# Placing the first pass over the third last chunk between the two negations of the last big chunk, in an elementwise kernel on one core

## The chip, the cores and the metric

One core of a Trainium2 chip. The metric is the device time of one execution in microseconds; lower is better. Most executions of a kernel here agree within about 2 us.

## The reference

```python
pred = np.clip(pred, 1e-7, 1 - 1e-7)                # both inputs 8192 x 8192, float32
return -(target * np.log(pred) + (1 - target) * np.log(1 - pred))   # target is 0 or 1
```

Since the target is 0 or 1, the kernel computes |t - 1 + p|, which is p or 1 - p, takes one logarithm and negates it.

## The kernel before

The data are cut into 37 chunks of 128 partitions. Chunks 2 to 33 hold 15360 elements per partition; 0, 1, 34 and 35 hold half of that (7680); 36 holds 2048. Two big places in a ring for pred (which is overwritten by the result) and for target take turns. A front is a clip and a subtraction on VectorE, then abs and logarithm on ScalarE; a back is the negation on VectorE. Big chunks are worked in two halves. In the profiles L82 is the clip, L85 the subtraction, L88 the abs, L89 the logarithm, L93 the negation, L74 and L78 the issue of a pred load and of a store. All engines run their instructions in the order of the program.

```python
def load(k):
    queue = nc.sync if k == 0 else nc.gpsimd
    nc.gpsimd.dma_start(out=spot(ring_t, k), in_=chunk(target, k))     # casts to bf16
    queue.dma_start(out=spot(ring_p, k), in_=chunk(pred, k))

def store(k):
    queue = nc.sync if k >= n - 3 else nc.gpsimd
    queue.dma_start(out=chunk(out, k), in_=spot(ring_p, k))

def front(k, *part):
    p, t = spot(ring_p, k, *part), spot(ring_t, k, *part)
    nc.vector.tensor_scalar(out=p, in0=p, scalar1=EPS, scalar2=1 - EPS, op0=Alu.max, op1=Alu.min)
    nc.vector.scalar_tensor_tensor(out=p, in0=t, scalar=1.0, in1=p, op0=Alu.subtract, op1=Alu.add)
    nc.scalar.activation(out=p, in_=p, func=Act.Abs)
    nc.scalar.activation(out=p, in_=p, func=Act.Ln)

def back(k, *part):
    p = spot(ring_p, k, *part)
    nc.vector.tensor_scalar(out=p, in0=p, scalar1=-1.0, scalar2=None, op0=Alu.mult)

# ... the first chunks cut ...
for k in range(2, n - 3):                  # n = 37
    front(k, (0, 2)); front(k, (1, 2))     # on two lines in the kernel
    back(k, (0, 2));  back(k, (1, 2))
    # ... store(k) and the loads that follow it, for k < n - 4 ...
store(n - 4)
a, b, c = n - 3, n - 2, n - 1
front(a)
front(b, (0, 2)); front(b, (1, 2))
back(a); store(a)
front(c)
back(b); store(b)
back(c); store(c)
```

Of the kernel before, what the change touches and what calls it, by code (L numbers as in the profile page):

```python
# [1 line left out]

# [4 lines left out]

EPS = 1e-7





BIG = 15 * 1024
HALF = BIG // 2


def plan(total):

    n, last = divmod(total, BIG)  # L20
    assert n > 4 and 0 < last <= 2048
    spots = [(HALF, 0), (HALF, HALF)]
    spots += [(BIG, k % 2 * BIG) for k in range(1, n - 1)]
    end = (n - 1) % 2 * BIG
    return spots + [(HALF, end), (HALF, end + HALF), (last, 2 * BIG)]



@with_exitstack
def kernel(  # L30
    ctx: ExitStack,
    tc: tile.TileContext,
    pred: bass.AP,
    target: bass.AP,
    out: bass.AP,
):






    nc = tc.nc
    fp32 = mybir.dt.float32
    bf16 = mybir.dt.bfloat16
    Alu = mybir.AluOpType
    Act = mybir.ActivationFunctionType
    P = nc.NUM_PARTITIONS

    R, C = pred.shape  # L50
    spots = plan(R * C // P)
    n = len(spots)
    widths = [w for w, _ in spots]
    cols = [sum(widths[:k]) for k in range(n)]

    def chunk(ap, k):
        flat = ap.rearrange("r c -> (r c)")
        return flat[cols[k] * P : (cols[k] + widths[k]) * P].rearrange("(p w) -> p w", p=P)

    pool = ctx.enter_context(tc.tile_pool(name="rings", bufs=1))  # L60
    ring = [P, 2 * BIG + widths[-1]]
    ring_p = pool.tile(ring, fp32, name="ring_p", tag="ring_p")
    ring_t = pool.tile(ring, bf16, name="ring_t", tag="ring_t")
    warm = pool.tile([1, 8], fp32, name="warm", tag="warm")

    def spot(ring, k, part=(0, 1)):
        w, c = spots[k]
        i, m = part
        return ring[:, c + i * w // m : c + (i + 1) * w // m]

    def load(k):
        queue = nc.sync if k == 0 else nc.gpsimd
        nc.gpsimd.dma_start(out=spot(ring_t, k), in_=chunk(target, k))  # L73
# [8 lines that stand above are left out]
        nc.vector.tensor_scalar(  # L82
            out=p, in0=p, scalar1=EPS, scalar2=1 - EPS, op0=Alu.max, op1=Alu.min
        )
        nc.vector.scalar_tensor_tensor(  # L85
            out=p, in0=t, scalar=1.0, in1=p, op0=Alu.subtract, op1=Alu.add
# [6 lines that stand above are left out]
        nc.vector.tensor_scalar(out=p, in0=p, scalar1=-1.0, scalar2=None, op0=Alu.mult)  # L93

    with tc.manual_schedule():
        for k in range(3):
            load(k)
        nc.vector.memset(warm, 1.0)  # L98
        nc.scalar.activation(out=warm, in_=warm, func=Act.Ln)  # L99
        front(0)  # L100
        front(1)
        back(0)
        store(0)
        back(1)
        store(1)
        load(3)
        for k in range(2, n - 3):
            front(k, (0, 2))
            front(k, (1, 2))
            back(k, (0, 2))  # L110
            back(k, (1, 2))
            if k < n - 4:
                store(k)

                for j in range(k + 2, n if k == n - 5 else k + 3):
                    load(j)
        store(n - 4)
        a, b, c = n - 3, n - 2, n - 1
        front(a)
        front(b, (0, 2))  # L120
        front(b, (1, 2))
        back(a)
        store(a)
        front(c)
        back(b)
        store(b)
        back(c)
        store(c)


# [1 line left out]
_INS = ['pred', 'target']  # L132
_OUTS = [((8192, 8192), 'float32')]


# [23 lines left out]
```

## Time and profile before

| | before |
|---|---|
| time, median of 3 runs (later 6) | 1867.1 us (1867.5) |
| VectorE / ScalarE busy | 60% / 48% |
| moved to and from HBM | 805 MB, 432 GB/s |
| VectorE waiting for pred loads, whole run | 391.0 us |

How to read it: no compute engine is near full, and the DMA engines hardly rest until the last 17 us. So a wait of a compute engine costs time only if the DMA engines run dry for it. The page (the profile's summary), the busy shares by 2 us stretches and the timeline that carry this are shown in the prediction.

### The profile page before, as it was taken

The page shows a single profiled execution, that of the slowest core. Times are in us where ns is not written, and L with a number is a line of the kernel's source. Part 1 is how long each engine was busy: PE and PEld are TensorE (multiplying, and loading weights), DVE is VectorE, ACT ScalarE, POOL GpSimd, SP SyncE. Part 2 cuts the span into 40 slices and gives each one's busy share as a digit, 9 for nine tenths or more (in the row PEclk, how much of TensorE's full clock was granted, in tenths as well). Part 3 has the DMA queues.
Part 4 walks back from the last instruction along what each step waited for, and adds up shares of the span by engine and source line. Part 5 has one row for each costly group of instructions (what it writes and reads, how often), then busy time and mean ns, then how long its engine had stood idle before and what let it go on. Part 6 is the DMA issues. An engine that isn't in the chain of part 4 may idle for free.

```text
span 1865.4 us, 619 instructions
## 1 busy us (share of the span) xinstructions
DVE 1122.2 (60%) x210; ACT 899.9 (48%) x142; POOL 60.9 (3%) x111
## 2 busy tenths in 40 slices
DVE  4655767555576655557665555766555576755575
ACT  3345553335555334555543355553345555433556
POOL 0000000000000000000000000000000000000010
DMA  9999999999999999999999999999999999999998
GB/s 295 376 358 340 357 341 365 387 379 353 344 353 353 359 387 381 351 353 345 353 360 387 385 350 353 345 353 361 383 386 349 354 350 345 362 383 387 356 329 379
DMA packets 15988, 671.13 MB, mean 360 GB/s; under 512 B 1776, under 2 KB 1776, under 8 KB 1904
## 3 DMA queue, kind: packets, MB, share of 16 engines
q0 software_dynamic: 15408, 658.25, 98.4%
q1 hardware_dynamic: 576, 12.85, 1.7%
q14 instruction: 4, 0.03, 0.0%
HBM read 536.87 MB, written 268.44 MB: 432 GB/s over the span
## 4 chain that ended last, share of the span: by engine, by line
DMA 36%; ACT 24%; issue 23%; DVE 16%; POOL 1%; DVEq 0%; POOLq 0%; PEldq 0%
DMA ring_p<-in_pred_dram 33%; ACT ring_p L88 12%; ACT ring_p L89 12%; DVE ring_p L85 8%; DVE ring_p L82 4%; DVE ring_p L93 4%; DMA out_dram<-ring_p 3%; POOL ring_t L73 0%; POOL out_dram L78 0%; DVEq L154 0%; POOLq L78 0%; DVEq L85 0%; PEldq L154 0%; POOLq L74 0%; POOLq L73 0%
## 5 line engine op out<-in xcount | busy, mean ns | idle before, releaser
L88 ACT ACTIVATE ring_p<-ring_p 128x7680 f32<-128x7680 f32 (+1 forms) x70 | 450.6, 6437 | 948.2 <-DVE ring_p L85 948.2
L85 DVE SCALAR_TENSOR_TENSOR ring_p<-ring_t,ring_p 128x7680 f32<-128x7680 bf16 (+1 forms) x70 | 557.2, 7960 | 2.4
L82 DVE TENSOR_SCALAR ring_p<-ring_p 128x7680 f32<-128x7680 f32 (+1 forms) x70 | 284.0, 4057 | 391.0 <-DMA ring_p<-in_pred_dram 391.0
L93 DVE TENSOR_SCALAR ring_p<-ring_p 128x7680 f32<-128x7680 f32 (+1 forms) x69 | 284.0, 4117 | 336.2 <-ACT ring_p L89 336.2
L89 ACT ACTIVATE ring_p<-ring_p 128x7680 f32<-128x7680 f32 (+1 forms) x70 | 451.1, 6444 | 2.2
L78 POOL DMA_DIRECT2D out_dram<-ring_p x34 | 21.6, 635 | 841.0 <-DVE ring_p L93 841.0
L74 POOL DMA_DIRECT2D ring_p<-in_pred_dram x36 | 19.3, 535 | 909.5 <-DMA out_dram<-ring_p 909.5
L73 POOL DMA_DIRECT2D ring_t<-in_target_dram x37 | 20.3, 550 | 0.8 <-PEq L154 0.8
L99 ACT ACT_TABLE_LOAD x1 | 1.3, 1283 | 0.7 <-PEq L143 0.7
L98 DVE MEMSET warm<- 1x8 f32 x1 | 0.1, 65 | 0.8 <-PEq L143 0.8
L99 ACT ACTIVATE warm<-warm 1x8 f32<-1x8 f32 x1 | 0.2, 208 | 0.0
L143 POOL MEMSET const-float32-0.0<- 128x1 f32 x1 | 0.1, 98 | 0.2 <-issue 0.2
L143 POOL MEMSET const-bfloat16-1.0<- 128x1 bf16 x1 | 0.1, 101 | 0.0
L143 POOL MEMSET const-float32-1.0<- 128x1 f32 x1 | 0.1, 98 | 0.0
L143 POOL MEMSET const-uint8-127<- 128x1 uint8 x1 | 0.1, 98 | 0.0
## 6 DMA issues: line engine op xcount, KB each, us to landing
ring_p<-in_pred_dram POOLq DMA_DIRECT2D x32, 7680.0 KB, 35.9
out_dram<-ring_p POOLq DMA_DIRECT2D x32, 7680.0 KB, 29.2
ring_t<-in_target_dram POOLq DMA_DIRECT2D x32, 3840.0 KB, 46.8
ring_p<-in_pred_dram POOLq DMA_DIRECT2D x3, 3840.0 KB, 35.0
ring_t<-in_target_dram POOLq DMA_DIRECT2D x4, 1920.0 KB, 27.6
out_dram<-ring_p POOLq DMA_DIRECT2D x2, 3840.0 KB, 27.6
out_dram<-ring_p SPq DMA_DIRECT2D x2, 3840.0 KB, 12.2
ring_p<-in_pred_dram SPq DMA_DIRECT2D x1, 3840.0 KB, 18.6
```

The source lines that it names most:

```text
L73: nc.gpsimd.dma_start(out=spot(ring_t, k), in_=chunk(target, k))
L74: queue.dma_start(out=spot(ring_p, k), in_=chunk(pred, k))
L78: queue.dma_start(out=chunk(out, k), in_=spot(ring_p, k))
L82: nc.vector.tensor_scalar(out=p, in0=p, scalar1=EPS, scalar2=1 - EPS, op0=Alu.max, op1=Alu.min)
L85: nc.vector.scalar_tensor_tensor(out=p, in0=t, scalar=1.0, in1=p, op0=Alu.subtract, op1=Alu.add)
L88: nc.scalar.activation(out=p, in_=p, func=Act.Abs)
L89: nc.scalar.activation(out=p, in_=p, func=Act.Ln)
L93: nc.vector.tensor_scalar(out=p, in0=p, scalar1=-1.0, scalar2=None, op0=Alu.mult)
L98: nc.vector.memset(warm, 1.0)
L99: nc.scalar.activation(out=warm, in_=warm, func=Act.Ln)
L143: nc = _bacc.Bacc("TRN2", target_bir_lowering=False, num_devices=1)
```

## The change

Its intent: VectorE has nothing to do while ScalarE finishes the second half of chunk 33. Let it do the front of 34 in that time, so that ScalarE gets the last chunks sooner and the last stores start sooner. The memset of a warm-up tile also moves ahead of the loads.

```diff
     with tc.manual_schedule():
+        nc.vector.memset(warm, 1.0)
         for k in range(3):
             load(k)
-        nc.vector.memset(warm, 1.0)
@@
-        for k in range(2, n - 3):
+        for k in range(2, n - 4):
@@ (store(k) and its loads lose their condition)
-        store(n - 4)
-        a, b, c = n - 3, n - 2, n - 1
+        z, a, b, c = range(n - 4, n)
+        front(z, (0, 2))
+        front(z, (1, 2))
+        back(z, (0, 2))
         front(a)
+        back(z, (1, 2))
+        store(z)
         front(b, (0, 2))
```

More of the change, by code (lines that the diff above doesn't have):

```diff
@@ L111 @@
             back(k, (1, 2))
-            if k < n - 4:
-                store(k)
-                for j in range(k + 2, n if k == n - 5 else k + 3):
-                    load(j)
-        store(n - 4)
-        a, b, c = n - 3, n - 2, n - 1
+            store(k)
+            for j in range(k + 2, n if k == n - 5 else k + 3):
+                load(j)
+        z, a, b, c = range(n - 4, n)
+        front(z, (0, 2))
+        front(z, (1, 2))
+        back(z, (0, 2))
         front(a)
+        back(z, (1, 2))
+        store(z)
         front(b, (0, 2))
```

## The prediction

> **What bounds the kernel now.** I read the page first: the busy shares, the 40 slices, then the end of the timeline, then the DMA transfers and their busy share by stretch.
>
> ```profile
> DVE 1122.2 (60%) x210; ACT 899.9 (48%) x142; POOL 60.9 (3%) x111
> DMA  9999999999999999999999999999999999999998
> HBM read 536.87 MB, written 268.44 MB: 432 GB/s over the span
> ```
>
> No compute engine is more than 60% busy, while the DMA row shows a nine in every slice but the last. The data are fixed (805 MB), so the kernel is bound by its 16 DMA engines, and a reordering of VectorE can only win what the DMA engines lose by standing idle. The place to look is the end, where the last digit is an 8. The busy share by 2 us stretches shows one hole:
>
> ```profile
> 1848.00:1850.00 2.00, 2.00 (x1) 1.97 (x2) 0.00 (x0) 1.00 0.36 154
> 1850.00:1852.00 2.00, 2.00 (x2) 1.06 (x1) 0.00 (x0) 1.00 0.04 15
> 1852.00:1854.00 2.00, 0.65 (x1) 0.00 (x0) 0.00 (x0) 1.00 1.17 492
> ```
>
> The last two columns are DMA share and GB/s. After it the stores of the last two chunks run at full rate to the end. Why the hole is there shows in the timeline:
>
> ```profile
> 1797.53 6.60 ACT L89 ACTIVATE ring_p<-ring_p 128x7680 f32<-128x7680 f32 x1
> 1804.17 4.16 DVE L93 TENSOR_SCALAR ring_p<-ring_p 128x7680 f32<-128x7680 f32 x1 [8.97 <-ACT ring_p L89]
> 1808.24 4.15 DVE L82 TENSOR_SCALAR ring_p<-ring_p 128x7680 f32<-128x7680 f32 x1
> 1808.62 3.90 POOL L78 DMA_DIRECT2D out_dram<-ring_p  x1 [22.23 <-DVE ring_p L93]
> 1812.43 8.16 DVE L85 SCALAR_TENSOR_TENSOR ring_p<-ring_t,ring_p 128x7680 f32<-128x7680 bf16 x1
> 1820.62 6.61 ACT L88 ACTIVATE ring_p<-ring_p 128x7680 f32<-128x7680 f32 x1 [16.49 <-DVE ring_p L85]
> ...
> 1847.35 5.29 DVE L93 TENSOR_SCALAR ring_p<-ring_p 128x7680 f32<-128x7680 f32 x2 [5.84 <-ACT ring_p L89]
> ```
>
> Chunks count from 0 to 36: 33 is the last big one, 34 and 35 the halves (third and second last), 36 the small one. VectorE idles 8.97 us for ScalarE before the second negation of 33, and only then begins 34; ScalarE idles 16.49 us for that, and is then busy without a break to the end of 36. So the negation of 35 comes only at 1847.35 to 1851.51, its store reaches the engines at 1852.37, and DMA engines that finished earlier had nothing to do.
>
> How much of the hole counts is a question of the single DMA engine. The trace's DMA records show fixed packet times (61440 B of store 33: 2.267 us; 30720 B of stores 34 and 35: 1.138; 8192 B of store 36: 0.31), eight packets of each transfer per engine, and a steady lag between the engines: p36 (the pred load of chunk 36) completes on the first engine at 1820.25 and on the last at 1824.63. At the hole most engines run out at 1848.1, others near 1850, the last at 1851.53. The mean idle per engine is about 3.3 us (from 0.36 and 0.04 over four microseconds, 3.2), but for the last engine it is 1852.37 - 1851.53 = 0.84 us.
>
> **What the Trainium skill says.** "DMA: Bandwidth & Descriptors", Issuing engines are not separate DMA queues: DMAs of all issuers run on the same 16 engines. The trace agrees: store 34, on the SyncE queue, interleaves with store 33, on the GpSimd one, from 1838.9, and the sum stays at 16 engines. So an earlier store adds no bandwidth; it only fills idle time. "SBUF — State Buffer", Who interferes with whom: a VectorE `tensor_scalar` in its two-port mode and a GpSimd access lock each other out for a whole instruction, which delays the descriptors of GpSimd's DMAs. The trace agrees: the issue of store 33 took 3.90 us, to 1812.52, just after the clip ended at 1812.39, where an issue beside the two-input subtraction took 0.53 (1783.75). This matters, since the change moves that issue. "Perfetto Trace Analysis", What "DMA-bound" means, lists as one bound the specific DMA engines; the lag above is of that kind, and it sets how much of the hole pays.
>
> **The change part by part.** The warm-up memset moves ahead of the loads in the program, but it is on VectorE and they are on other queues; it ran at 0.80 us, long before the first data at 19.3. Worth 0. Splitting the loop at k = n - 4 adds and removes no instruction. What is left is one swap on VectorE: front(34) before the second negation of 33.
>
> I re-run the end with the measured durations. VectorE ends the first negation of 33 at 1795.2. front(34) needs p34, issued at 1783.75 and landed 17.8 us later:
>
> ```profile
> ring_p<-in_pred_dram POOLq DMA_DIRECT2D x1, 3840.0 KB, 17.8
> ```
>
> That is 1801.6, so the new first wait is on a load, 6.4 us, inside the 8.97 us that VectorE idled anyway. Clip 1801.6 to 1805.8, subtraction to 1814.0. Then the second negation of 33, whose ScalarE input was ready at 1804.13: 1813.9 to 1818.1, where before it ended at 1808.3. The store of 33 is issued at about 1818.4 instead of 1808.62, and its descriptors are written by about 1819 instead of 1812.5, since the next clip can start only when p35 lands at 1819.8 and does not lock GpSimd out.
>
> Does that late store cost? The GpSimd queue drains in order, and the loads of 34 to 36 stand ahead of it. The first engine came to store 33 at 1819.9, the last finished p36 at 1824.3. Descriptors ready at 1819 to 1821 may leave the early engines idle for up to a microsecond or so; the late ones, which set the end, don't wait. Cost on the path: 0.
>
> What the earlier front(34) gives: ScalarE starts 34 at 1814.0 instead of 1820.62 and ends it at 1827.2 instead of 1833.9. Front(35) first half waits for p35: 1819.8 to 1826.1; second half to 1832.4, only 0.7 earlier than before. Negation of 34: 1832.4 to 1836.5, store issued at 1836.6 instead of 1838.08. ScalarE has 35 at 1827.2 to 1840.6 without a gap (four passes of 3.4), so the negation of 35 runs 1840.7 to 1844.8 instead of 1847.35 to 1851.51: 6.7 us earlier. 36 follows: ScalarE to 1844.4, negation by 1846.0. Both last stores are thus in the queue before the first engine runs out at 1848.1, and the hole closes.
>
> The gain is what the last engine idled. Its work from the landing of p36 on: 8 x 2.267 (store 33) + 8 x 1.138 (34) + 8 x 1.138 (35) + 8 x 0.3135 (36) = 18.14 + 9.10 + 9.10 + 2.51 = 38.85 us, so 1824.63 + 38.85 = 1863.5. As a check the same sum for 33 and 34 alone gives 1851.87, and store 34 landed at 1851.88. Store 36 landed at 1864.56 before, so 1.1 us less by this sum; 0.84 by the idle time alone. I take 0.95: 1867.1 - 0.95 = 1866.15, rounded to 1866.2. The 6.7 us won on ScalarE are nearly all hidden behind the transfers.
>
> **The rivals.** *The whole hole pays.* If engines shared one limit, so that late ones sped up when early ones rest, the mean idle of 3.3 us would be won: 1863.8. Against it: a packet of 30720 B takes 1.138 us (median of 1.141 on the SyncE queue), full house or not, and the lag among the engines stands at 4.4 us from 515 us on and never closes. *The late store of 33 opens a hole of its own.* GpSimd's first transfer was issued at 1.23 us and its first packet ran at 5.57, so up to 4.3 us from issue to packet on an empty queue: 1818.4 + 4.3 = 1822.7, still 1.6 us before the last engine is free. But if the issue collides with the clip of 35 (to 1822.0) on top of that, packets start near 1826 and the last engine loses about 2 us; less the 0.95 won, that makes 1868.2. For it: 3.90 us for that very issue before. Against it: 1.4 us between the issue and the landing of p35. *Nothing at all:* where the lag of the last engine happens to meet the store, or run-to-run spread (1866.34 to 1867.97 before) swallows it: 1867.1.
>
> **Range and chances.** The spread of before is as large as the gain. I centre on 1866.2 and go from 1864.6 (half of the hole paying, with a fast run) to 1867.8 (gain lost to a collision or a slow draw). 2% is 37 us; the hole is 3.3 and the whole stretch that the change touches lasts 60, all but the hole filled with transfers. So within 2% is all but certain.
>
> **What would show it.** After the change: VectorE's wait before the clip of 34 is on p34, about 6.4 us, and ScalarE's wait of 16.49 shrinks to about 10; store 33 issued near 1818.4 in about half a microsecond; store of 35 issued near 1845; no stretch under 0.9 DMA share from 1848 to 1854; end of the span near 1864.4. I am wrong in mechanism if the issue of store 33 takes microseconds again with a dip of DMA share near 1821 to 1824 that reaches the last engine, or if p34 lands later than 1802. I am wrong in size if the engines' lag at the end is gone and the span falls by 3 us.

## More of the kernel before

One more view before, the sums of waits from 1780 us on, is of use for the comparison (waiting line, what it waited for, us in total, times, longest):

```profile
ACT ring_p L88 <- DVE ring_p L85: 44.5, 2, 28.0
...
POOL out_dram L78 <- DVE ring_p L93: 22.2, 1, 22.2
DVE ring_p L93 <- ACT ring_p L89: 16.6, 4, 9.0
```

VectorE's line has no wait for a load there: it waits for ScalarE's logarithms instead, 16.6 us.

## The result, and the profile after

1865.84 us, median of 6 runs (1865.15 to 1866.23), against 1867.5 (1866.34 to 1868.11) for 6 runs of before. A ratio here is the mean time of one kernel's runs over that of the other's of the same rounds, so not quite the ratio of the medians quoted; it is 0.9991 with a 95% interval from 0.9978 to 1.0004. The six times of the changed kernel all lie below the six of before, so a small gain is likely, but the interval doesn't exclude none, and what the gain comes from can't be told from the times. The traces tell it.

The stretches of the changed kernel at the place of the hole (the last two columns are DMA share and GB/s):

```profile
1848.00:1850.00 2.00, 0.00 (x0) 0.00 (x0) 0.00 (x0) 1.00 1.07 461
1850.00:1852.00 2.00, 0.00 (x0) 0.00 (x0) 0.00 (x0) 1.00 1.03 445
1852.00:1854.00 2.00, 0.00 (x0) 0.00 (x0) 0.00 (x0) 1.00 0.89 384
```

DMA share of 0.36 and 0.04 has become 1.07 and 1.03: the hole is closed. (A share can pass 1, or fall to 0.89 with no engine idle, since the profile counts the whole of a packet in the stretch in which it starts.) Its timeline:

```profile
1801.49 4.16 DVE L82 TENSOR_SCALAR ring_p<-ring_p 128x7680 f32<-128x7680 f32 x1 [6.53 <-DMA ring_p<-in_pred_dram]
1805.69 8.16 DVE L85 SCALAR_TENSOR_TENSOR ring_p<-ring_t,ring_p 128x7680 f32<-128x7680 bf16 x1
1813.76 4.15 DVE L93 TENSOR_SCALAR ring_p<-ring_p 128x7680 f32<-128x7680 f32 x1
1813.88 6.61 ACT L88 ACTIVATE ring_p<-ring_p 128x7680 f32<-128x7680 f32 x1 [9.98 <-DVE ring_p L85]
1818.21 0.54 POOL L78 DMA_DIRECT2D out_dram<-ring_p  x1 [31.94 <-DVE ring_p L93]
1819.62 2.16 DVE L82 TENSOR_SCALAR ring_p<-ring_p 128x3840 f32<-128x3840 f32 x1 [1.70 <-DMA ring_p<-in_pred_dram]
...
1840.62 5.29 DVE L93 TENSOR_SCALAR ring_p<-ring_p 128x7680 f32<-128x7680 f32 x2 [0.85 <-ACT ring_p L89]
```

The first line is the clip of 34, now waiting for its load and not behind a negation; the third is the delayed second negation of 33, and the fifth the store of 33, issued 9.6 us later than before but in 0.54 us instead of 3.90. The last line, the negations of 35 and 36, starts at 1840.62 instead of 1847.35. The sums of waits from 1780 us on:

```profile
ACT ring_p L88 <- DVE ring_p L85: 38.0, 2, 28.0
POOL out_dram L78 <- DVE ring_p L93: 31.9, 1, 31.9
...
DVE ring_p L82 <- DMA ring_p<-in_pred_dram: 8.2, 2, 6.5
DVE ring_p L93 <- ACT ring_p L89: 1.9, 2, 1.0
```

VectorE traded 16.6 us of waiting for ScalarE for 1.9, plus 8.2 of waiting for loads, and ScalarE's wait fell by 6.5. The last negation came 6.7 us sooner, the end 1.35.

For the end, one number is finer than the time of a run, and I use it from here on as **the last stretch**: from the moment that the load of pred 36 has landed on all DMA engines to the moment that the store of 36 has, by the completion records of the trace. The DMA work before it is common to the two kernels. It is 39.92 us before (1824.64 to 1864.56) and 38.76 after (1824.44 to 1863.21): 1.16 us less. The profile's own line for store 36 (KB, us from issue to landing), before (issued at 1852.68) and after (issued at 1845.94):

```profile
out_dram<-ring_p SPq DMA_DIRECT2D x1, 1024.0 KB, 11.9
out_dram<-ring_p SPq DMA_DIRECT2D x1, 1024.0 KB, 17.3
```

The rest of the 1.35 us, 0.19, is when pred 36 landed, which differs by chance from run to run. The mean idle of a DMA engine, counted from the packets in flight between 1818 us and 3.5 us before the last landing, went from 3.57 us to 0 (3.25 of the 3.57 in the hole; 0.32 near 1838.5, before store 34 starts, which the prediction passed over). That is the point to be explained: 3.57 us of idle went, and 1.16 came out.

The completion records show where the rest went. Store 36 landed on the first and the last engine 0.21 us apart before and 3.03 us apart after: the hole of before had only made the early engines wait for the late ones. (The records don't name a packet's engine. The last engine's end of work is read from the last packet to end and the last of the 16 landings.)

### The profile page after: what moved, and what is told of

Its sections match the earlier page's. It is cut to its first block, busy times and chain, and to the rows that moved or that the text cites. A ratio compares the mean times of both kernels' runs of the same rounds, so it can differ in the third digit from the quotient of the medians.

```text
span 1864.1 us, 619 instructions
## 1 busy us (share of the span) xinstructions
DVE 1122.2 (60%) x210; ACT 899.9 (48%) x142; POOL 57.5 (3%) x111
## 4 chain that ended last, share of the span: by engine, by line
DMA 35%; issue 26%; ACT 22%; DVE 15%; POOL 1%; DVEq 0%; POOLq 0%; PEldq 0%
DMA ring_p<-in_pred_dram 32%; ACT ring_p L88 11%; ACT ring_p L89 11%; DVE ring_p L85 7%; DVE ring_p L82 4%; DVE ring_p L93 4%; DMA out_dram<-ring_p 3%; POOL ring_t L73 0%; POOL out_dram L78 0%; DVEq L157 0%; POOL ring_p L74 0%; POOLq L78 0%; POOLq L73 0%; DVEq L82 0%; PEldq L157 0%
## 5 line engine op out<-in xcount | busy, mean ns | idle before, releaser
L82 DVE TENSOR_SCALAR ring_p<-ring_p 128x7680 f32<-128x7680 f32 (+1 forms) x70 | 284.0, 4057 | 399.0 <-DMA ring_p<-in_pred_dram 399.0
L74 POOL DMA_DIRECT2D ring_p<-in_pred_dram x36 | 19.3, 535 | 909.2 <-DMA out_dram<-ring_p 909.2
```

## The experiments

The theory: the 16 DMA engines each have the same fixed work, and the one that lags most, "the last engine", sets the end. Idle time of the others costs nothing. The changed kernel's records fit this: the seven last landings of pred 36, in order, lie 38.70 to 38.77 us before the seven last of store 36; the nine earlier ones, which don't set the end, 39.05 to 39.77. The rivals: the mean idle pays (engines share a limit); the chain through ScalarE sets the end; the memset has a part. All kernels below gave correct results. Each was timed in 5 rounds, in three calls on different chips; the table has the median, that of the kernel before in the same call (9 runs), and the last stretch, the mean idle and the spread of the engines at the landing of pred 36, from the one profiled execution. Mean idle is a lower bound, since up to 21 packets were in flight on 16 engines; and in halves_before 0.39 and in halves_after 0.81 of it are early engines at the very end, with all their work done.

| run | time, us | before, us | last stretch, us | mean idle, us | spread, us |
|---|---|---|---|---|---|
| before | 1867.5 | | 39.92 | 3.57 | 4.4 |
| after | 1865.84 | 1867.5 | 38.76 | 0.00 | 4.0 |
| memset_only | 1867.22 | 1867.21 | 39.90 | 3.06 | 3.8 |
| swap_only | 1866.23 | 1867.21 | 38.77 | 0.00 | 3.3 |
| halves_before | 1866.03 | 1867.21 | 38.76 | 0.49 | 4.5 |
| halves_after | 1865.88 | 1867.21 | 38.77 | 2.09 | 7.2 |
| halves_after_again | 1866.35 | 1867.47 | 38.71 | 0.00 | 3.4 |
| late35_5us | 1866.16 | 1867.3 | 38.79 | 1.97 | 4.2 |
| late35_8us | 1869.25 | 1867.3 | 41.80 | 4.95 | 3.9 |
| late33_2us | 1866.28 | 1867.3 | 38.77 | 1.47 | 4.2 |
| late33_4us | 1866.82 | 1867.3 | 39.93 | 2.70 | 3.2 |
| sync_stores | 1961.15 | 1867.47 | (other order) | | 9.6 (1.0 at store 33) |

Except for sync_stores every interval of a ratio includes 1: each is about 0.13% wide on either side, and a microsecond is 0.05%. So the verdicts below rest on the last stretch, which came out at 38.71 to 38.79 in the seven profiles where the theory says that the last engine never waits.

### memset_only and swap_only: the change taken apart

```diff
 # memset_only, against before
+        nc.vector.memset(warm, 1.0)
         for k in range(3):
             load(k)
-        nc.vector.memset(warm, 1.0)
```

```diff
 # swap_only, against after
-        nc.vector.memset(warm, 1.0)
         for k in range(3):
             load(k)
+        nc.vector.memset(warm, 1.0)
```

> The kernel before with the memset moved ahead of the loads and nothing else. Theory (the gain is all in the swap on VectorE): same as before, 0 +- 0.4 us; from the last landing of the pred load of chunk 36 to the last landing of store 36 about 39.9 us as before, and the hole in the DMA records at 1848 to 1852 is there unchanged. Rival (the earlier memset starts the whole pipeline earlier): about 1 us faster, with that stretch still 39.9.

> The changed kernel with the memset put back behind the loads, so the swap alone. Theory: as the changed kernel, about 1.2 us faster than before; the stretch from the last landing of pred 36 to that of store 36 about 38.8 us and no hole. Rival (the memset gives part of it): less than 0.8 us faster.

Measured: memset_only is the kernel before (last stretch 39.90, hole there), swap_only is the changed kernel (38.77, no hole). The stretches of memset_only:

```profile
1848.00:1850.00 2.00, 2.00 (x1) 1.97 (x2) 0.00 (x0) 1.00 0.47 200
1850.00:1852.00 2.00, 2.00 (x2) 1.13 (x1) 0.00 (x0) 1.00 0.07 31
```

By the last stretch, all of it is the swap on VectorE; the times are too scattered to split 1 us.

### halves_before and halves_after: the same lead for ScalarE by another way

```diff
 # halves_before against before; halves_after against after
-        front(a)
+        front(a, (0, 2))
+        front(a, (1, 2))
```

> The kernel before, order on VectorE unchanged, but front(34) in two halves, so that ScalarE starts 34 about 6 us earlier (near 1814.5) while the store of 33 is issued as early as before. Theory (an earlier ScalarE closes the hole; the place of the second negation does not matter by itself): store 35 reaches the queue near 1846, the hole closes, stretch from pred 36 to store 36 about 38.8 us, 1.1 us faster than before. Rival (the swap itself, the later store of 33, is what gains): no change, 39.9 us.

> The changed kernel with front(34) in two halves on top, so ScalarE starts 34 about 12 us earlier than before. Theory (with the hole closed the last DMA engine is busy without a break, nothing is left to win): as the changed kernel within 0.3 us, stretch 38.8 us, although the last negation ends earlier or the same. Rival (the end is still set by the chain of ScalarE): another 1 us or more.

Measured, halves_before: 38.76 us, the same as the changed kernel's, without moving the store of 33. Its timeline:

```profile
1808.71 2.15 DVE L82 TENSOR_SCALAR ring_p<-ring_p 128x3840 f32<-128x3840 f32 x1
1809.09 1.90 POOL L78 DMA_DIRECT2D out_dram<-ring_p  x1 [22.21 <-DVE ring_p L93]
1810.90 4.16 DVE L85 SCALAR_TENSOR_TENSOR ring_p<-ring_t,ring_p 128x3840 f32<-128x3840 bf16 x1
1814.97 2.15 DVE L82 TENSOR_SCALAR ring_p<-ring_p 128x3840 f32<-128x3840 f32 x1
1815.09 3.40 ACT L88 ACTIVATE ring_p<-ring_p 128x3840 f32<-128x3840 f32 x1 [10.49 <-DVE ring_p L85]
```

ScalarE starts 34 at 1815.09 after 10.49 us of idling, nearly as in the changed kernel (9.98), though the order of VectorE is that of before. So what gains is ScalarE's earlier start, and with it the earlier store of 35 (issued at 1846.34), and not the place of the negation. (The store's issue, blocked by a clip of half the width, took 1.90 us and not 3.90.)

halves_after gained nothing more, as the theory has it: with the hole closed nothing is left there. But its profiled execution was the slowest of its five, 1869.58 us against 1865.54 to 1866.05, with pred 36 landing at 1828.03, 3.6 us later than in the changed kernel, and the engines 7.2 us apart. Its last stretch was 38.77 all the same. That fits the theory from another side: a larger lag of the last engine, built up over the run (6.2 us of spread by 916 us, before any line that the edit touches), went into the time nearly one for one. Whether the edit could have caused it was tested by taking it again:

> The changed kernel with front(34) in two halves, as before: the profiled execution of the first take was the slowest of its five (1869.58 against 1865.54 to 1866.05 for the others) and its records show the DMA engines 7.2 us apart by the end, against 4.0 in the changed kernel, from upstream of the edit. Theory (that is chance in the long middle part, and the last engine's lag there goes one for one into the time): the spread at pred 36 is back at 3 to 5 us, the stretch from pred 36 to store 36 stays 38.8 us, time 1865.5 to 1866.5. Rival (the halves cause it): the spread is 6 us or more again.

Measured: spread 3.4 us, last stretch 38.71, median 1866.35. So the halves don't bring that lag with them; what made it in the first take is not known.

### late35_5us and late35_8us: making the hole again, to measure

```diff
 # against after; again() multiplies a chunk or part of it by 1 in place, on VectorE
+        again(b)
+        again(b, (0, 4))            # late35_8us: again(b) here instead
         back(b)
         store(b)
```

> The changed kernel with 5.3 us of idle work on VectorE (a multiplication by 1 of chunk 35) just before the negation of 35. Stores 35 and 36 then reach the DMA engines near 1851, when most engines have been out of work for 2 to 2.5 us and only the last ones are still busy. Theory (the last engine sets the end): 0 to +0.2 us against the changed kernel, stretch from the last landing of pred 36 to that of store 36 38.8 to 39.0 us, with a mean idle per engine near 2 us. Rival (the mean idle pays): about +2 us, stretch near 40.7.

> The same with 8.3 us of idle work. Stores 35 and 36 reach the engines near 1854, about 2.6 us after the last engine ran out. Theory: +2.5 us against the changed kernel, stretch 41.3 us, i.e. a slope of 1 from where the last engine runs out, though mean idle per engine is then near 5 us. Rival (mean idle pays): +5 us, stretch near 43.7.

The stretches of late35_5us:

```profile
1848.00:1850.00 2.00, 2.00 (x1) 0.00 (x0) 0.00 (x0) 1.00 0.32 138
1850.00:1852.00 2.00, 1.47 (x2) 0.00 (x0) 0.00 (x0) 1.00 0.64 276
```

and of late35_8us:

```profile
1848.00:1850.00 2.00, 1.97 (x2) 0.00 (x0) 0.00 (x0) 1.00 0.22 92
1850.00:1852.00 2.00, 2.00 (x1) 0.00 (x0) 0.00 (x0) 1.00 0.04 15
1852.00:1854.00 2.00, 2.00 (x2) 0.00 (x0) 0.00 (x0) 1.00 0.14 61
```

The first has a hole of 1.97 us per engine, more than half of the hole of before, and costs 0.03 us in the last stretch (38.79): the rival of the mean idle, which asked for 40.7, falls. (The records of before say the same: in the hole the nine packets of store 34 that started after 1848.8, with most engines idle, took 1.138 us each, as with all engines busy.) The second adds 3.00 us of delay to the store, 3.01 to the stretch and 3.09 to the median time. Its expectation (41.3) was 0.5 short, for two reasons: the last engine idled 2.73 us (1851.25 to 1853.98) where I had said 2.6, and the stretch grew by 3.04 against the changed kernel, so 0.31 us come on top of the idle. The kernel before shows the same surplus: idle of the last engine 0.85 us (1851.52 to 1852.37), stretch 1.16 longer. So when all engines restart at once, about 0.3 us are lost beyond the idle as I count it. The records show part of it: the second round of packets took 1.196 us instead of 1.138, once (0.06); and I count idle to the first packet of store 35, while the 16 first packets start over 0.15 us (1852.37 to 1852.52 in before), so the last engine may have idled up to 0.15 longer. The rest stays open.

### late33_2us and late33_4us: the price of the late store

```diff
 # against after
         front(a)
+        again(z, (2, 4))            # late33_4us: again(z, (1, 2))
         back(z, (1, 2))
         store(z)
```

> The changed kernel with 2.15 us of idle work ahead of the second negation of 33, so the store of 33 is issued near 1820.3, when pred 35 has landed and the next clip starts at once. Theory: the issue is blocked by that clip and takes about 2 us instead of 0.54, packets of store 33 start near 1823 to 1824, early engines idle for 3 us, the last engine (free at 1824.1) hardly: stretch 38.8 to 39.1 us, time +0 to +0.3 against the changed kernel. Rival (the idle of the early engines pays): +2 us.

> The same with 4.16 us of idle work: issue of store 33 near 1822.4, blocked until the clip ends near 1824.4, packets from 1825 to 1826. Theory: the last engine now idles 1 to 2 us and the end moves by just that: stretch 39.8 to 40.8 us, +1 to +2 against the changed kernel. Rival (early engines' idle pays): +4 to +5 us. Rival (late stores cost nothing since the hole at the end takes it up): 0.

The issue and the clip beside it, first of late33_2us:

```profile
1820.42 2.15 DVE L82 TENSOR_SCALAR ring_p<-ring_p 128x3840 f32<-128x3840 f32 x1
1820.80 1.90 POOL L78 DMA_DIRECT2D out_dram<-ring_p  x1 [34.21 <-DVE ring_p L93]
```

then of late33_4us:

```profile
1821.40 2.15 DVE L82 TENSOR_SCALAR ring_p<-ring_p 128x3840 f32<-128x3840 f32 x1
1821.78 1.90 POOL L78 DMA_DIRECT2D out_dram<-ring_p  x1 [36.21 <-DVE ring_p L93]
```

Both issues are held until the clip is over: 1821.78 + 1.90 = 1823.68, 0.13 us after the clip's end at 1823.55. (The Trainium skill, "SBUF — State Buffer", A bandwidth-pool intuition that's wrong, gives a blocked issue as the end of the VectorE instruction plus about 115 ns. Agrees; in the kernel before it was 0.13 us too, clip to 1812.39, issue to 1812.52.) The first packet of store 33 follows 0.57 us after the end of the issue in both (1823.27 and 1824.25). In late33_2us the last engine finishes pred 36 at 1824.54, after that, and does not wait: stretch 38.77 in spite of 1.47 us mean idle. In late33_4us it finishes at 1823.52 and waits 0.73 us (1 to 2 were expected): stretch 39.93, 1.17 more, of which 0.4 is again beyond the idle. Here the late store costs just what the whole change gains, and the hole at the end no longer takes it up. The changed kernel has the store's packets ready at about 1819.3 (1818.75 + 0.57), some 4.8 us before its last engine needs them (1824.14); In both runs the collision with the clip adds to the idle work: the issue ends 3.95 us later than in the changed kernel in late33_2us, which was free, and 4.93 later in late33_4us, which was not. The 4.8 lie between.

### sync_stores: another queue

```diff
 # against after
     def store(k):
-        queue = nc.sync if k >= n - 3 else nc.gpsimd
-        queue.dma_start(out=chunk(out, k), in_=spot(ring_p, k))
+        nc.sync.dma_start(out=chunk(out, k), in_=spot(ring_p, k))
```

> The changed kernel with every store issued on the SyncE queue instead of the last three only. Loads and stores are then in two queues that the DMA engines interleave, and the GpSimd queue no longer waits for a store's place. Question: does the lag of the last engine (4 us by the end, most of it from the first 500 us) belong to having one queue, and can it be had back? If so, spread below 2 us at the end and 1 to 3 us faster than the changed kernel. Theory as it stands (the total is fixed packet times on engines that never rest, the lag comes from rare long packets whatever queue they are in): spread 3 to 5 us, time within 1 us of the changed kernel, or slower if the stores now push the loads back and VectorE starves.

Measured: 1961.15 us, 5% slower than before (ratio 1.0503, interval 1.0488 to 1.0517). The spread at pred 36 itself was 9.6 us: its packets of 8192 B then run beside those of store 33, which is in the other queue. At the transfers around it (loads of pred 34 and 35, stores 33 to 36) the spread did fall, to 0.9 to 1.0 us, but at a price far above it. From the page of this run, VectorE's wait for the pred loads, and that of the issue of these loads for a store (the number after the last arrow is the idle time, in us, put down to that releaser):

```profile
L81 DVE TENSOR_SCALAR ring_p<-ring_p 128x7680 f32<-128x7680 f32 (+1 forms) x70 | 284.0, 4058 | 498.8 <-DMA ring_p<-in_pred_dram 498.5
...
L74 POOL DMA_DIRECT2D ring_p<-in_pred_dram x36 | 30.0, 834 | 1657.9 <-DMA out_dram<-ring_p 1559.7
```

In the changed kernel these were 399.0 and 909.2. And 573 of the 4096 pred load packets of 61440 B took longer than 2.3 us, where the changed kernel has 77 in 8192 loads and stores. The sum of what they took over 2.267 us is 32 us per engine, of the 94 that its span is longer than the changed kernel's; how the rest splits between waiting and order was not followed up. As a way to win back the lag, this is closed; the expectation of "within 1 us" missed, its "or slower" held.

No version beat the changed kernel: every kernel that closes the hole lies at the same last stretch, and what is left (the spread of 3 to 4 us) is made long before the lines of this change.

## Why the prediction was right

By its own steps:

- **The bound.** Held. The DMA engines set the end; the compute engines' waits moved by 6 to 15 us and the end by 1.35.
- **The new wait of VectorE on pred 34.** 6.4 us said, 6.53 measured, inside idle time; ScalarE's wait 9.98 where about 10 was said.
- **The store of 33.** Issue near 1818.4 in half a microsecond: 1818.21 in 0.54. No DMA engine idled for it: mean idle 0.00.
- **Closing the hole.** Negations of 35 from 1840.7: 1840.62. No DMA share below 0.9 up to 1854 was asked; the last of the three stretches has 0.89, with no engine idle by the packets in flight, so that sign was set too narrow.
- **The size.** The one term with a choice in it. I had 0.84 us by the last engine's idle and 1.1 by the sum of packet times (38.85 us for the last stretch), and took 0.95. The sum was right: the stretch is 38.76. The idle time alone fell short by the 0.3 us that come on top of it at a restart (late35_8us, and before). By the medians of 6 runs the gain was 1.66, by those of swap_only and halves_before 0.98 and 1.18; the spread of runs is as large. So that the median came within 0.4 us of the predicted 1866.2 is in part luck: the 1867.1 that it was reckoned from, a median of 3 runs, became 1867.5 with 6.
- **The rivals.** The mean idle of 3.3 us pays: refuted by late35_5us. The collision of the late store with the clip: real, as late33_4us shows, and it did not happen in the changed kernel, because the issue ended 0.9 us before the clip. One figure in this rival was wrong: 4.3 us from issue to first packet, taken from the first transfer of the run. On a warm queue that had run dry it is 1.1 us (halves_after, issue at 1821.46, packet at 1822.58).

## What to carry to other kernels

Where DMA engines are the bound, ask of a hole how long the engine that lags most stands idle in it, and not how wide it is on average: 1.97 us of mean idle cost 0.03 here, while 0.85 us on the last engine cost 1.16. A compute reordering is worth only the part of its lead that such an engine would have waited (1.16 of 6.7 us), and two quite different reorderings that give ScalarE the same lead are worth the same. When a gain is smaller than the scatter of the times, look for a stretch of the trace that leaves the scatter out.

## What the Trainium skill lacked or had wrong

- "DMA: Bandwidth & Descriptors", Issuing engines are not separate DMA queues, says that DMAs of all issuers run on the same engines (seen here too) and that issuing from several saves only issue time. The choice of the queue can cost much more than it saves: all stores on the SyncE queue took 1961.15 us against 1867.47 for the kernel before (1865.84 for the changed kernel), with longer waits for the loads and longer load packets; the cause was not isolated.
- The same page, Latency and other measured facts, says that some DMA engines are usually slower in traces. It doesn't say that a lag builds up among them in the first part of a run and then stays. In the kernel before the spread of the landings of one transfer grows from 0.8 us (at 58 us) to 4.4 us (at 479 us) and then stays; of 71 packets of 61440 B above 2.3 us (up to 3.49 where 2.267 is usual) 56 fall in the first 500 us. In other executions it came to 3.2 to 7.2 us. That the engines drift apart until their packets no longer meet would fit, but it was not tested.
- No page has the cost of a restart of all engines at once: 0.3 to 0.4 us beyond the idle as counted here (before, late35_8us, late33_4us), explained only in part.
- "DMA: Bandwidth & Descriptors", Specifications, has about 1 us to the first byte for DMAs from GpSimd. Agrees on a warm queue (1.1 us from the start of the issue to the first packet), but the first one of a run took 4.3 us (1.23 to 5.57 in before; the first packet came at 5.55 to 5.80 in all twelve traces), which I found on no page.
